# Written instruction order at the sublayer boundaries of a two-layer conditioned trunk

## The chip, the cores and the metric

The kernel runs on one core of a Trainium2 chip. The metric is device time in microseconds (us): the median of the runs shown. The profile is of one execution, with its own time.

## The reference, cut to what matters

Two layers, each three sublayers: a SwiGLU feed-forward (ffn), a token mixer (layer 0: the HGRN2 recurrence, "hg"; layer 1: a chunked gMLP, "gm"), and another ffn. 256 tokens, width 1024, ffn width 2816, all float32.

```python
def sublayer(x, fn, pre_g, post_g, shift, scale, gate, res_w):
    h = rms_norm(x, pre_g) * (1.0 + scale) + shift
    return x + res_w * gate * rms_norm(fn(h), post_g)

cond = jax.nn.silu(c)
for i in range(DEPTH):
    mod = (cond @ ada_w[i] + ada_b[i])      # 9 vectors of 1024: shift, scale, gate of 3 sublayers
    for s in range(N_SUB):
        x = sublayer(x, fns[s], norm_pre[i, s], norm_post[i, s],
                     mod[:, 3*s], mod[:, 3*s+1], mod[:, 3*s+2], (0.5, 1.0, 0.5)[s])
```

Between two sublayers lies a chain that no matmul of the next one can pass: norm of the product y, residual, norm of x, scale and shift to the next h.

## The kernel before, in words

**Tiles.** The 256 tokens are two tiles t of 128 rows. Every product is taken as three matmuls on float32 values split in a high and a low part: high by high, high by low, low by high. Activations h are kept transposed: h2[high or low, t, 128-column chunk].

**Weights.** They stream in as 188 blocks of two halves of 512 KB. A half is loaded by SyncE (SP) into a `raw` tile (four buffers), ScalarE (ACT) casts it to the high part (line 119, "the cast"), VectorE (DVE) subtracts that for the low part (line 120, "the sub"); both land in `whl` tiles (12 buffers). `next_block()` calls `wblock()` one or two blocks ahead of use.

**Ada.** The conditioning product is 144 column loads of 512 KB. Each is reduced against `cond` on DVE (line 169) into one column of `mod`. `pace()` gives each sublayer a number of blocks over which its share of these is spread.

**Units.** An ffn is 11 units of 256 columns: two input products, silu times product, a split in high and low, then the output product accumulated in y[t][h] (four PSUM banks, h the half of the width). `out_last()` does the output product of the last three units, 18 matmuls for each t and h; in hg it has 12. In hg, after the projections, `gate_f` (line 529 on) makes the decays in a tile `L`, a tree of levels fills the scores (lines 570 to 599), and the finish norms each head (lines 645 to 668: `ss`, `ots`) and multiplies by the output weights.

**The boundary.** `tail(t)` squares y (line 216, ACT), takes the root (line 79) and the reciprocal (line 224, DVE), multiplies y by the gate G (lines 259, 263), adds it to x (line 265). `nxt(t)` squares x, and `prenorm` scales it to `xn` (line 233 on DVE, 235 on ACT), transposes it on TensorE (PE) into `npa` (line 239), applies scale and shift on ACT in float32 (line 243), and splits it on DVE: a cast for the high part (line 247) and a subtraction for the low (line 248). Then `proj` (line 291 and on) starts the next sublayer. The boundaries are called B1 (ffn0 to hg), B2 (hg to ffn1), B3 (ffn1 to ffn2), B4 (ffn2 to gm) and B5 (gm to ffn3).

**Order.** `tile.TileContext(nc)` schedules the instructions of each engine; program order and tile dependences go in, and each engine runs its list in that order, one behind the other. Loads go out on SP's queue in program order.

Of the kernel before, what the change touches and what calls it, by code (L numbers as in the profile page):

```python
# [33 lines left out]
class Body:  # L34
    def __init__(self, ctx, tc, ins, out):
# [5 lines left out]
        self.whl = pool("whl", 12)  # L41
        self.act = pool("act", 1)
        self.adap = pool("adap", 2)
# [68 lines left out]
    def wblock(self, ap, n=2048):  # L112
        nc = self.nc
        hi, lo = self.wtile(), self.wtile()
        for h in range(2):
            sl = slice(h * n // 2, (h + 1) * n // 2)
            raw = self.raw.tile([P, 1024], F32, tag="raw", name="raw")[:, 0:n // 2]
            self.load(raw, ap[:, sl])
            nc.scalar.copy(hi[:, sl], raw)  # L119
            nc.vector.tensor_sub(lo[:, sl], raw, hi[:, sl])  # L120
        self.credit += self.rate
        while self.credit >= 1:
            self.credit -= 1
            self.ada(min(self.ada_next + 1, self.limit))
        return hi, lo

    def next_block(self):

        while len(self.ready) <= self.ahead and self.blk < len(self.blocks):
            self.ready.append(self.wblock(*self.blocks[self.blk]))  # L130
            self.blk += 1
        return self.ready.pop(0)
# [18 lines left out]
    def ada_setup(self):  # L151
        nc = self.nc
        self.ada_next = 0
        self.pace(0, 1)
        self.mod = [self.const.tile([P, 24], F32, name=f"mod{i}") for i in range(6)]
        self.cond = self.const.tile([P, D], F32, name="cond")
        self.ring = 0

    def ada(self, upto):
        nc = self.nc  # L160
        while self.ada_next < min(upto, 144):
            i = self.ada_next
            if self.ring and i % 3:
                t = self.p4.tile([P, D], F32, tag="t4", name="ada")
            else:
                t = self.adap.tile([P, D], F32, tag="ada", name="ada")
            self.load(t, self.d["ada"][i])
            junk = self.scr.tile([P, D], BF16, tag="junkv", name="junkv")
            nc.vector.tensor_tensor_reduce(junk, t, self.cond, 1.0, 0.0, ALU.mult, ALU.add,  # L169
                                           self.mod[i // 24][:, i % 24:i % 24 + 1])  # L170
# [38 lines left out]
    def rstd(self, src, second):  # L209

        nc = self.nc
        s2 = self.tiny.tile([P, 2], F32, tag="s2", name="s2")
        be = self.tiny.tile([P, 1], F32, tag="be", name="be")
        for h in range(2):
            junk = self.scr.tile([P, 512], BF16, tag="junka", name="junka")
            nc.scalar.activation(junk, src[h], AF.Square, accum_out=s2[:, h:h + 1])
            if h == 0:
                nc.vector.tensor_scalar(be, s2[:, 0:1], 1.0 / D, EPS, op0=ALU.mult, op1=ALU.add)
                if second is not None:
                    second()  # L220
        r = self.tiny.tile([P, 1], F32, tag="r", name="r")
        sq = self.tiny.tile([P, 1], F32, tag="sq", name="sq")
        self.tact(sq, s2[:, 1:2], AF.Sqrt, scale=1.0 / D, bias=be)
        nc.vector.reciprocal(r, sq)
        return r

    def prenorm(self, t, hT, A, sh, r):
        nc = self.nc
        xn = self.scr.tile([P, D], F32, tag="xn", name="xn")
        for h in range(2):  # L230
            hs = slice(h * 512, (h + 1) * 512)
            if h == 0:
                nc.vector.tensor_scalar(xn[:, hs], self.x[t][:, hs], r, None, op0=ALU.mult)
            else:
                nc.scalar.activation(xn[:, hs], self.x[t][:, hs], AF.Copy, scale=r)
            pa = self.yps.tile([P, 512], F32, tag=f"y{t}{h}", name="npa")
            for k in range(4):
                kc = 4 * h + k
                nc.tensor.transpose(pa[:, k * P:(k + 1) * P], xn[:, kc * P:(kc + 1) * P], self.ident)
            hf = self.scr.tile([P, 512], F32, tag="hf", name="hf")  # L240
            for k in range(4):
                kc = 4 * h + k
                nc.scalar.activation(hf[:, k * P:(k + 1) * P], pa[:, k * P:(k + 1) * P],
                                     AF.Identity, bias=sh[:, kc:kc + 1], scale=A[:, kc:kc + 1])
            hv = hf.rearrange("p (k t) -> p k t", k=4)
            hs4 = slice(4 * h, 4 * h + 4)
            nc.vector.tensor_copy(hT[0][:, t, hs4, :], hv)  # L247
            nc.vector.tensor_sub(hT[1][:, t, hs4, :], hv, hT[0][:, t, hs4, :])

    def tail(self, t, y, G, mm, nxt, last=False):  # L250

        nc = self.nc
        yg = self.scr.tile([P, D], F32, tag="yg", name="yg")
        xt = self.x[t]
        hs = [slice(0, 512), slice(512, D)]
        mm(t, 0)

        def second():
            nc.vector.tensor_mul(yg[:, hs[0]], y[t][0], G[:, hs[0]])
            mm(t, 1)  # L260

        r = self.rstd(y[t], second)
        nc.vector.tensor_mul(yg[:, hs[1]], y[t][1], G[:, hs[1]])
        for h in range(2):
            nc.vector.scalar_tensor_tensor(xt[:, hs[h]], yg[:, hs[h]], r, xt[:, hs[h]], op0=ALU.mult, op1=ALU.add)
            if last:
                self.load(self.out[t][:, hs[h]], xt[:, hs[h]])
        nxt(t)
# [10 lines left out]
    def proj(self, hT, wbs, n, split=False, kper=4):  # L279

        res = [[self.acc.tile([P, 512], F32, tag="acc", name="pps")[:, 0:n] for t in range(NT)] for _ in wbs]

        def go(g, t, blk):
            w = wbs[g][blk]
            ks = [blk * kper + k for k in range(kper)]
            h = lambda i, kc: hT[i][:, t, kc, :]
            u = lambda i, kc: w[i][:, (kc - ks[0]) * n:(kc - ks[0] + 1) * n]
            mm = self.nc.tensor.matmul
            if split:
                for kc in ks:  # L290
# [805 lines left out]
```

## Time and profile before

| what | value |
|---|---|
| runs | 1189.97, 1191.43, 1196.67 us; median 1191.43 |
| profiled execution | 1193.24 us, its span 1191.5 us |
| mean granted TensorE clock | 0.984 |
| PE, DVE, ACT busy | 96%, 75%, 55% of the span |
| moved by DMA | 282.32 MB, 237 GB/s over the span |

In a row of the table of windows stand the stretch, its length, then the busy time of each engine with its number of instructions, the granted TensorE clock (PEclk, 1.00 is full), the DMA share and rate. A row of the waits has the engine and what it wanted to do, what it waited for, the total in us, how often, and the longest. A row of the timeline has start and duration in us, engine, line, operation, output and input tiles, and in brackets the idle time before it with what ended it. A row of a group ends with total busy us, mean ns of one, and the idle time before it.

### The profile page before, as it was taken

How to read it: one execution, taken by the hardware profiler on the slowest of the kernel's cores; microseconds unless marked ns; L12 is line 12 of the kernel's file. 1: busy time of each engine (PE TensorE's matmuls, PEld its weight loads, DVE VectorE, ACT ScalarE, POOL GpSimd, SP SyncE). 2: the span in 40 equal slices, each digit the busy share in tenths (PEclk: the TensorE clock that was granted, in tenths of full speed). 3: DMA queues.
4: the chain of work that ended last, by engine and by line, in shares of the span. 5: the costliest groups of instructions: out<-in, count | busy, mean ns of one | idle time of the engine just before them, and what ended most of it. 6: DMA issues, size and time to landing. Idle time of an engine off the chain costs nothing.

```text
span 1191.5 us, 17180 instructions
## 1 busy us (share of the span) xinstructions
PE 1146.5 (96%) x6518; PEld 995.4 (84%) x6518; DVE 888.8 (75%) x1331; ACT 657.2 (55%) x1054; POOL 6.8 (1%) x16
## 2 busy tenths in 40 slices
PE   7999999997997999999999999999999999999997
PEld 6999998797895788888778888888888887888886
DVE  6997888868887887787677787657978786666652
ACT  6464446648766754456655545554754457555541
POOL 0000000000000000000000000000000000000000
PEclk9999999997999999999999999999999999999999
DMA  9899998782335777887578888537777765666640
GB/s 345 311 314 318 333 327 314 251 285 101 124 95 185 263 267 272 278 272 262 173 251 267 282 269 272 188 124 261 277 254 262 248 212 177 203 222 233 213 137 36
DMA packets 79765, 282.32 MB, mean 237 GB/s; under 512 B 9873, under 2 KB 10561, under 8 KB 79682
## 3 DMA queue, kind: packets, MB, share of 16 engines
q1 hardware_dynamic: 78626, 278.05, 68.0%
q0 software_dynamic: 1056, 3.17, 0.8%
q8 instruction: 51, 0.84, 0.3%
q14 instruction: 32, 0.26, 0.1%
HBM read 280.11 MB, written 1.07 MB: 236 GB/s over the span
## 4 chain that ended last, share of the span: by engine, by line
PE 73%; DMA 10%; DVE 8%; ACT 5%; issue 3%; SPq 0%; DVEq 0%; ACTq 0%
PE ups L328 15%; PE ups L329 8%; PE y L144 7%; PE y L142 7%; PE y L143 7%; PE ups L418 4%; DMA ada<-in_ada 4%; DMA raw<-in_wffn 4%; DVE w L120 3%; PE ups L334 3%; PE ups L336 3%; PE ups L335 3%; DMA raw<-in_whg 3%; ACT w L119 2%; PE ab L599 2%
## 5 line engine op out<-in xcount | busy, mean ns | idle before, releaser
L120 DVE TENSOR_TENSOR w<-raw,w 128x1024 fp32r<-128x1024 f32 x376 | 453.5, 1220 | 84.7 <-ACT w L119 77.5
L119 ACT CAST w<-raw 128x1024 fp32r<-128x1024 f32 x376 | 388.0, 1050 | 202.9 <-DMA raw<-in_wffn 79.4
L328 PE MATMUL ups<-h,w 128*128 128x512 f32 x864 | 303.1, 394 | 0.0
L169 DVE CUSTOM_DVE_ANT_0 junkv<-ada,cond 128x1024 bf16<-128x1024 f32 x144 | 175.8, 1221 | 92.0 <-DMA ada<-in_ada 91.5
L329 PE MATMUL ups<-h,w 128*128 128x256 f32 x864 | 242.5, 281 | 0.0
L328 PEld LDWEIGHTS ups<-h,w 128*128 128x128 f32 x864 | 162.3, 188 | 36.8
L142 PE MATMUL y<-w,t 128*128 128x512 f32 x448 | 179.4, 400 | 4.5 <-ACT t L147 4.5
L143 PE MATMUL y<-w,t 128*128 128x512 f32 x448 | 178.2, 398 | 0.0
L144 PE MATMUL y<-w,t 128*128 128x512 f32 x448 | 177.6, 397 | 0.2
L329 PEld LDWEIGHTS ups<-h,w 128*128 128x128 f32 x864 | 163.7, 190 | 0.9
L334 PE MATMUL ups<-h,w 128*128 128x256 f32 x416 | 118.3, 285 | 0.6 <-ACT w L119 0.6
L336 PE MATMUL ups<-h,w 128*128 128x256 f32 x416 | 117.8, 283 | 0.2 <-DVE w L120 0.2
L335 PE MATMUL ups<-h,w 128*128 128x256 f32 x416 | 117.6, 283 | 0.0
L142 PEld LDWEIGHTS y<-w,t 128*128 128x128 f32 x448 | 84.5, 189 | 24.1 <-ACT t L147 5.3
L144 PEld LDWEIGHTS y<-w,t 128*128 128x128 f32 x448 | 84.3, 189 | 21.0 <-DVE t L148 1.1
L143 PEld LDWEIGHTS y<-w,t 128*128 128x128 f32 x448 | 84.5, 189 | 17.9
L79 ACT ACTIVATE t<-t 128x256 f32<-128x256 f32 (+2 forms) x70 | 36.3, 523 | 97.7 <-DVE t L378 95.5
L334 PEld LDWEIGHTS ups<-h,w 128*128 128x128 f32 x416 | 79.7, 192 | 1.7 <-ACT w L119 0.8
L335 PEld LDWEIGHTS ups<-h,w 128*128 128x128 f32 x416 | 79.7, 192 | 0.8 <-issue 0.2
L336 PEld LDWEIGHTS ups<-h,w 128*128 128x128 f32 x416 | 79.7, 192 | 0.4 <-DVE w L120 0.4
L291 PE MATMUL pps<-w,h 128*128 128x512 f32 x160 | 64.4, 403 | 5.3 <-DVE h L247 5.3
L292 PE MATMUL pps<-w,h 128*128 128x512 f32 x160 | 63.8, 399 | 0.0
(199 smaller groups left out, 1435.4 us busy)
## 6 DMA issues: line engine op xcount, KB each, us to landing
raw<-in_wffn SPq DMA_DIRECT2D x264, 512.0 KB, 5.5
ada<-in_ada SPq DMA_DIRECT2D x144, 512.0 KB, 6.5
raw<-in_wgmu SPq DMA_DIRECT2D x48, 512.0 KB, 5.2
raw<-in_whg SPq DMA_DIRECT2D x40, 512.0 KB, 5.8
raw<-in_wgmv SPq DMA_DIRECT2D x24, 512.0 KB, 5.0
G<-gflat POOLq DMA_DIRECT2D x6, 512.0 KB, 5.9
t<-in_gbin SPq DMA_DIRECT2D x6, 256.0 KB, 5.2
x<-in_x SPq DMA_DIRECT2D x2, 512.0 KB, 4.0
```

The lines of the kernel that those rows point to most:

```text
L119: nc.scalar.copy(hi[:, sl], raw)
L120: nc.vector.tensor_sub(lo[:, sl], raw, hi[:, sl])
L142: self.paced(mm(ps, l[0], r[0], start=start, stop=False))
L143: mm(ps, l[0], r[1], start=False, stop=False)
L144: mm(ps, l[1], r[0], start=False, stop=stop)
L169: nc.vector.tensor_tensor_reduce(junk, t, self.cond, 1.0, 0.0, ALU.mult, ALU.add, self.mod[i // 24][:, i % 24:i % 24 + 1])
L291: mm(res[g][t], h(0, kc), u(0, kc), start=kc == 0, stop=False)
L328: self.paced(mm(ps, u[0], self.h2[:, :, :, kc, :], start=kc == 0, stop=False))
L329: mm(ps[:, 1, :], u[1], self.h2[:, 0, :, kc, :], start=False, stop=kc == KC - 1)
L334: self.paced(mm(o, u[0], h[0], start=start, stop=False))
L335: mm(o, u[0], h[1], start=False, stop=False)
L336: mm(o, u[1], h[0], start=False, stop=stop)
```

## The change

- All scheduling is done with `schedule_with_timeline_sim=True`. The five boundaries are written out by hand in `boundary()`, in a region in which ACT, DVE and PE keep the written order; `close()` ends it within the next sublayer. `tail()` remains for the end of the kernel.
- A weight half is now a `cast()` and a `sub()` that can be placed apart. `boundary()` sets four halves ahead of the last product of t0 (0, 0), two more between its halves, one cast and sub, and one more half, in t1's chain. Casts, subs and ada reduces that come later in the program are kept behind the last `h_high` and `h_low` by `hold`.
- ACT writes the high part of h directly from `npa` (`h_high`). DVE computes scale and shift again in float32, in four pieces of 128 columns, and subtracts (`h_low`).
- `proj` gives two lists, one for each tile, high by high and high by low first. The first 30 matmuls of t0 stand ahead of t1's transposes. In an ffn the first unit is interleaved with them (`first_units`).
- Ada loads are issued up to three reduces ahead at the start and have three buffers. `whl` has 14 buffers, and the reduce writes in place. `L` has a pool of its own. The paces go from 25 and 26 blocks to 23 and 22.
- In the finish of hg, by the order that results, the twelve output matmuls that stood behind the last heads' product `ab` on PE now stand ahead of it.

```diff
-        self.whl = pool("whl", 12)
+        self.whl = pool("whl", 14)
-        self.adap = pool("adap", 2)
+        self.adap = pool("adap", 3)
+        self.lp = pool("lp", 1)
...
+    def cast(self):
+        if self.half is None:
+            self.half = [self.wtile(), self.wtile(), 0]
+        hi, lo, h = self.half
+        ap, n = self.blocks[self.blk]
+        sl = slice(h * n // 2, (h + 1) * n // 2)
+        raw = self.raw.tile([P, 1024], F32, tag="raw", name="raw")[:, 0:n // 2]
+        self.load(raw, ap[:, sl])
+        self.after(self.nc.scalar.copy(hi[:, sl], raw), self.hold[0])
+        self.casts.append((hi, lo, sl, raw, h))
...
+    def sub(self):
+        hi, lo, sl, raw, h = self.casts.pop(0)
+        self.after(self.nc.vector.tensor_sub(lo[:, sl], raw, hi[:, sl]), self.hold[1])
...
+    def halves(self, n=1):
+        for _ in range(n):
+            self.cast()
+            self.sub()
...
-            junk = self.scr.tile([P, D], BF16, tag="junkv", name="junkv")
-            nc.vector.tensor_tensor_reduce(junk, t, self.cond, 1.0, 0.0, ALU.mult, ALU.add,
-                                           self.mod[i // 24][:, i % 24:i % 24 + 1])
+            for j in range(len(self.ada_tiles), min(i + (1 if self.ring else 3), 144)):
...
+                self.load(t, self.d["ada"][j])
+                self.ada_tiles.append(t)
+            t = self.ada_tiles[i]
+            self.after(nc.vector.tensor_tensor_reduce(t, t, self.cond, 1.0, 0.0, ALU.mult, ALU.add,
+                                                      self.mod[i // 24][:, i % 24:i % 24 + 1]), self.hold[1])
...
+    def h_high(self, t, h, xn, cols):
...
+        for k in range(4):
+            kc = 4 * h + k
+            last = nc.scalar.activation(self.h2[:, 0, t, kc, :], pa[:, k * P:(k + 1) * P], AF.Identity,
+                                        bias=sh[:, kc:kc + 1], scale=A[:, kc:kc + 1])
+        return pa, last
+
+    def h_low(self, t, h, pa, cols):
...
+        for k in range(4):
+            kc, ks = 4 * h + k, slice(k * P, (k + 1) * P)
+            nc.vector.tensor_scalar(hf[:, ks], pa[:, ks], A[:, kc:kc + 1], sh[:, kc:kc + 1],
+                                    op0=ALU.mult, op1=ALU.add)
+        hs4 = slice(4 * h, 4 * h + 4)
+        return nc.vector.tensor_sub(self.h2[:, 1, t, hs4, :], hf.rearrange("p (k t) -> p k t", k=4),
+                                    self.h2[:, 0, t, hs4, :])
...
+    def boundary(self, y, G, mm, cols, table):
+        self.region = self.tc.manual_schedule(engines={E.Activation, E.DVE, E.PE})
+        self.region.__enter__()
...
+        self.halves(4)
+        sy, sx, yg = self.row_stats(), self.row_stats(), ytile()
+        do(mm(0, 0))
+        sq(0, 0, sy)
+        self.half_mean(sy)
+        gated(0, 0, yg)
+        self.halves(2)
+        do(mm(0, 1))
+        sq(0, 1, sy)
+        gated(0, 1, yg)
+        r = self.inv_rms(sy)
+        self.residual(0, yg, r, sx)
+        r = self.inv_rms(sx)
+        do(mm(1, 0))
...
+        self.scaled(0, 0, xn, r)
+        sq(1, 0, sy1)
+        self.scaled(0, 1, xn, r)
+        self.half_mean(sy1)
+        gated(1, 0, yg1)
+        self.alloc_h()
+        m = mm(1, 1)
+        do(m[0:3])
+        pa0, _ = self.h_high(0, 0, xn, cols)
+        do(m[3:4])
+        pa1, _ = self.h_high(0, 1, xn, cols)
+        do(m[4:])
+        self.h_low(0, 0, pa0, cols)
+        self.h_low(0, 1, pa1, cols)
+        w = [[self.ready.pop(0) for _ in range(2)] for _ in range(2)]
+        self.res, go = self.proj(w)
+        sq(1, 1, sy1)
+        gated(1, 1, yg1)
+        r = self.inv_rms(sy1)
+        self.cast()
+        self.residual(1, yg1, r, sx1)
+        self.sub()
+        r = self.inv_rms(sx1)
...
+        self.halves(1)
+        p0 = go(0)
+        do(p0[0:30])
+        pa0, _ = self.h_high(1, 0, xn, cols)
...
+        self.table(table)
+        self.hold = (act, dve)
+        self.first = go(1)
...
-            L = self.adap.tile([P, 512], F32, tag="ada", name="L")
+            L = self.lp.tile([P, 512], F32, tag="L", name="L") if pr else self.scr.tile([P, 512], F32, tag="hf", name="L")
...
-    with tile.TileContext(nc) as tc:
+    with tile.TileContext(nc, schedule_with_timeline_sim=True) as tc:
```

What the change moves is seen in the lists of the engines. At the start of the kernel, on DVE before (the ISA rows are reduces: of x0 and x1 for the first norm, then of ada columns; `xn` and `yg` are the two tiles of normed x):

```order
L905 ISA xn,s_125<-x_99 128x1024
L905 ISA s_125 128x1
L905 ISA yg,s_125<-x_100 128x1024
L905 ISA s_125 128x1
L928 TENSOR_SCALAR ab_167<-adab 128x8
L907 TENSOR_SCALAR v<-s_125 128x2
L909 RECIPROCAL r<-v 128x2
L915 TENSOR_SCALAR xn<-x_99,r 128x512
```

and after:

```order
L1052 ISA xn,s_128<-x_102 128x1024
L1052 ISA s_128 128x1
L192 ISA ada,mod_106<-ada,cond 128x1024
L192 ISA mod_106 128x1
L1054 TENSOR_SCALAR v<-s_128 128x2
L192 ISA ada,mod_106<-ada,cond 128x1024
L192 ISA mod_106 128x1
L1091 TENSOR_TENSOR shift<-mod_106,adab 128x1
L1056 RECIPROCAL r<-v 128x2
L1092 SCALAR_TENSOR_TENSOR A<-mod_106,ab_170,npre 128x1
L1062 TENSOR_SCALAR xn<-x_102,r 128x512
```

Two ada reduces now stand ahead of the reciprocal and of xn. On ACT two weight casts moved from behind the first h to between the copies of the transposed x, and a third ahead of that h.

At B1, on ACT before (the CAST of t is the high part of the last unit of ffn0, y_797 and y_798 are y00 and y01):

```order
L147 CAST t_2037<-t_2036 128x512
L73 ACT_TABLE_LOAD
L119 CAST w<-raw 128x1024 x3
L216 ACTIVATE junka,s_2123<-y_797 128x512
L119 CAST w<-raw 128x1024
L216 ACTIVATE junka,s_2123<-y_798 128x512
L79 ACTIVATE sq<-s_2123,be 128x1
```

and after (y_784 and y_785):

```order
L167 CAST t_2009<-t_2008 128x512
L74 ACT_TABLE_LOAD
L122 CAST w<-raw 128x1024 x8
L235 ACTIVATE junka,s_2091<-y_784 128x512
L122 CAST w<-raw 128x1024 x2
L235 ACTIVATE junka,s_2091<-y_785 128x512
L80 ACTIVATE sq<-s_2091,be 128x1
```

Eight casts stand ahead of the first square instead of three, and two ahead of the second instead of one.

At B3, on DVE before (y_4081 and y_4082 are y00 and y01; `be` is half of the mean square):

```order
L218 TENSOR_SCALAR be<-s_5481 128x1
L259 TENSOR_TENSOR yg<-y_4081,G 128x512
L169 ISA junkv,mod_106<-ada,cond 128x1024
L169 ISA mod_106 128x1
L224 RECIPROCAL r<-sq 128x1
L263 TENSOR_TENSOR yg<-y_4082,G 128x512
L265 SCALAR_TENSOR_TENSOR x_99<-yg,r,x_99 128x512 x2
L218 TENSOR_SCALAR be<-s_5514 128x1
L224 RECIPROCAL r<-sq 128x1
L233 TENSOR_SCALAR xn<-x_99,r 128x512
```

and after (y_4097 and y_4098):

```order
L242 TENSOR_SCALAR be<-s_5429 128x1
L310 TENSOR_TENSOR yg<-y_4097,G 128x512
L132 TENSOR_TENSOR w<-raw,w 128x1024 x2
L310 TENSOR_TENSOR yg<-y_4098,G 128x512
L248 RECIPROCAL r<-sq 128x1
L255 SCALAR_TENSOR_TENSOR x_102<-yg,r,x_102 128x512
L242 TENSOR_SCALAR be<-s_5433 128x1
L255 SCALAR_TENSOR_TENSOR x_102<-yg,r,x_102 128x512
L248 RECIPROCAL r<-sq 128x1
L293 TENSOR_SCALAR xn<-x_102,r 128x512
```

The ada reduce ahead of the reciprocal is gone, and two weight subs stand between the two products with the gate.

More of the change, by code (lines that the diff above doesn't have):

```diff
@@ L110, in wtile, with wblock @@
         return self.whl.tile([P, 2048], dt, tag="w", name="w")
[L112 to L120, printed above, removed]
+    def cast(self):
[8 more added lines that the diff above has]
+        self.casts.append((hi, lo, sl, raw, h))
+        if h:
+            self.half, self.blk = None, self.blk + 1
+        else:
+            self.half[2] = 1
+    def sub(self):
+        hi, lo, sl, raw, h = self.casts.pop(0)
+        self.after(self.nc.vector.tensor_sub(lo[:, sl], raw, hi[:, sl]), self.hold[1])
+        if h:
+            self.ready.append((hi, lo))
+    def halves(self, n=1):
+        for _ in range(n):
+            self.cast()
+            self.sub()
+    def wblock(self):
+        self.halves(2)
         self.credit += self.rate
@@ new lines, in half_mean, with inv_rms, residual @@
+    def half_mean(self, st):
+        self.nc.vector.tensor_scalar(st[1], st[0][:, 0:1], 1.0 / D, EPS, op0=ALU.mult, op1=ALU.add)
+    def inv_rms(self, st):
+        s2, be, sq, r = st
+        self.tact(sq, s2[:, 1:2], AF.Sqrt, scale=1.0 / D, bias=be)
+        self.nc.vector.reciprocal(r, sq)
+        return r
+    def residual(self, t, yg, r, st=None):
+        for h in range(2):
+            hs = slice(512 * h, 512 * h + 512)
+            self.nc.vector.scalar_tensor_tensor(self.x[t][:, hs], yg[:, hs], r, self.x[t][:, hs],
+                                                op0=ALU.mult, op1=ALU.add)
+            if st is None:
+                self.load(self.out[t][:, hs], self.x[t][:, hs])
+            else:
+                self.square(self.x[t][:, hs], st[0], h)
+                if h == 0:
+                    self.half_mean(st)
@@ L214, in rstd, with close, tail @@
+    def close(self):
+        for op in self.first:
+            op()
+        self.region.__exit__(None, None, None)
+    def tail(self, t, y, G, mm):
+        yg = self.scr.tile([P, D], F32, tag="yg", name="yg")
+        st = self.row_stats()
         for h in range(2):
-            junk = self.scr.tile([P, 512], BF16, tag="junka", name="junka")
-            nc.scalar.activation(junk, src[h], AF.Square, accum_out=s2[:, h:h + 1])
+            for op in mm(t, h):
+                op()
+            self.square(y[t][h], st[0], h)
@@ L217, in rstd @@
             if h == 0:
[L218 to L268, printed above, removed]
+                self.half_mean(st)
@@ L335, in mm3f @@
         mm(o, u[0], h[1], start=False, stop=False)
[L336 removed]
+        self.last = mm(o, u[1], h[0], start=False, stop=stop)
     def gtile(self):
@@ L345, in out_unit @@
             for h in range(2):
+                self.gate = self.last
                 for k in range(2):
@@ L399, in post_tok @@
                     self.split_ps(*[g[:, :, t * P:(t + 1) * P] for g in gTs[u]], pv[:, u])
-            return gTs
+            act(0)
+            self.halves(2)
+            do(self.first[0:30])
+            ps = turn(0)
+            split(0, ps)
+            do(self.first[30:])
+            act(1)
+            wa, wb = nb(), nb()
+            steps = unit2(wa, wb)
+            next(steps)
+            ps = turn(1)
+            split(1, ps)
+            pend.extend(gTs)
+            next(steps)
+            self.first = []
+            self.close()
+            return steps
         def out():
@@ L789, in gelu, with tok @@
             self.tact(o, o, AF.Gelu_apprx_tanh)
+        def tok(n):
+            res = [self.acc.tile([P, 512], F32, tag="acc", name="pps")[:, 0:n] for t in range(NT)]
+            for b in range(2):
+                w = nb()
+                for t in range(NT):
+                    for k in range(4):
+                        kc = 4 * b + k
+                        self.mm3(res[t], [a[:, t, kc, :] for a in hT], [u[:, k * n:(k + 1) * n] for u in w],
+                                 kc == 0, kc == KC - 1)
+            return res
         v, vt = [], []
@@ L955, in run @@
         self.blocks, self.blk, self.ready, self.ahead = [], 0, [], 0
+        self.half, self.casts, self.hold = None, [], (None, None)
         for src, n, k in ((d["wffn"][0], 2048, 33), (d["whg"], 2048, 20), (d["wffn"][1], 2048, 33),
```

188 lines of the change are left out of this document (109 added, 79 removed).

## The prediction

> **What bounds the kernel now.** I read the engine totals first, then the table of windows around the sublayer boundaries, then PE's waits, and last the timeline of the places that wait.
>
> ```profile
> PE 1146.5 (96%) x6518; PEld 995.4 (84%) x6518; DVE 888.8 (75%) x1331; ACT 657.2 (55%) x1054; POOL 6.8 (1%) x16
> 360.93 0.48 PE L142 MATMUL y<-w 128*128 128x512 f32 x1
> ...
> 363.52 0.39 PE L144 MATMUL y<-w 128*128 128x512 f32 x1
> ```
>
> PE is the bound, and the number of matmuls is the same before and after, so only stretches in which PE stands still, or runs at half clock, can be won. The last two rows are the first and the last of twelve: (363.52 - 360.93) / 11 = 0.235 us for each 512-wide matmul when PE is fed. That is the unit in which I count cover.
>
> The windows below hold, in this order, the boundaries ffn0 to hg (B1), the front of hg, its finish, then hg to ffn1 (B2), ffn1 to ffn2 (B3), ffn2 to gm (B4) and gm to ffn3 (B5).
>
> ```profile
> core 0: us, PE busy (x) PEld busy (x) DVE busy (x) ACT busy (x) POOL busy (x), PEclk, DMA share, GB/s
> 204.00:222.00 18.00, 14.57 (x71) 11.54 (x70) 15.95 (x28) 13.14 (x27) 0.00 (x0) 1.00 0.67 222
> 268.00:294.00 26.00, 19.31 (x110) 18.49 (x109) 21.51 (x37) 24.70 (x48) 0.00 (x0) 0.74 0.33 116
> 362.00:373.00 11.00, 6.47 (x24) 4.53 (x23) 9.09 (x18) 7.74 (x20) 0.00 (x0) 0.84 0.69 238
> 381.00:393.00 12.00, 9.09 (x30) 6.73 (x29) 11.19 (x20) 11.28 (x26) 0.00 (x0) 0.72 0.30 93
> 573.00:615.00 42.00, 36.54 (x155) 28.71 (x154) 32.73 (x53) 28.83 (x54) 0.00 (x0) 0.92 0.63 216
> 766.00:800.00 34.00, 33.91 (x156) 27.27 (x155) 22.50 (x38) 22.45 (x48) 0.00 (x0) 1.00 0.33 109
> 1005.00:1025.00 20.00, 17.58 (x83) 13.39 (x81) 12.38 (x16) 13.30 (x22) 0.00 (x0) 1.00 0.61 210
> 577.00:580.40 3.40, 3.40 (x13) 3.01 (x13) 2.41 (x4) 3.40 (x7) 0.00 (x0) 0.50 0.00 0
> ```
>
> I count a window's loss as its PE idle time plus busy time times (1 - PEclk), since busy time at half clock is half lost:
> - B1: 18.00 - 14.57 = 3.4.
> - hg front: 6.7 idle + 19.31 x 0.26 = 11.7.
> - hg finish: 4.5 + 6.47 x 0.16 = 5.6.
> - B2: 2.9 + 9.09 x 0.28 = 5.5.
> - B3: 5.5 + 36.54 x 0.08 = 8.4.
> - B4: 0.1. B5: 2.4.
>
> Together 37 us, 3% of the span, is all that order can win besides the start. What PE waited for in them:
>
> ```profile
> PE ots L663 <- DVE t L658: 4.4, 1, 4.4
> PE npa L239 <- DVE xn L233: 3.2, 2, 2.1
> PE fps L336 <- DVE w L120: 3.1, 2, 1.7
> PE tps L396 <- DVE t L393: 0.9, 1, 0.9
> ```
>
> All of these are waits for DVE. Weights (line L120) are late only in the hg front; elsewhere the wait is for a norm's chain or a unit's product.
>
> **The change, part by part.**
>
> *The boundary chain.* After the change it has a fixed order. Its length comes from these groups:
>
> ```profile
> L216 ACT ACTIVATE junka<-y 128x512 bf16<-128x512 f32 x24 | 14.4, 598 | 39.0 <-PE y L144 38.9
> L216 ACT ACTIVATION_READ_ACCUMULATOR junka<-y 128x1 f32 x24 | 4.8, 200 | 0.0
> L79 ACT ACTIVATE sq<-s,be 128x1 f32<-128x1 f32 x22 | 6.6, 301 | 1.2 <-DVE be L218 0.7
> L224 DVE RECIPROCAL r<-sq 128x1 f32<-128x1 f32 x22 | 3.5, 157 | 4.3 <-ACT sq L79 4.2
> L265 DVE SCALAR_TENSOR_TENSOR x<-yg,r,x 128x512 f32<-128x512 f32 x24 | 17.0, 746 | 0.2
> L233 DVE TENSOR_SCALAR xn<-x,r 128x512 f32<-128x512 f32 x10 | 4.8, 485 | 0.3
> ```
>
> From the end of y00 (18 matmuls for each tile and half in an ffn): y01 ends at 18 x 0.235 = 4.2; square and its read 0.8, root 0.3, reciprocal 0.16, two residual halves 1.5, the square of the second half 0.8 behind them, root and reciprocal 0.46, xn 0.49: 8.7, and with some 0.1 us for each of ten hand-overs 9.7. PE has work until 4.2 + (18 + 9) x 0.235 = 10.6. So with free engines the transposes find xn ready.
>
> *B3.* Before, the chain took longer for a reason that the timeline shows:
>
> ```profile
> 569.77 0.29 ACT L79 ACTIVATE sq<-s,be 128x1 f32<-128x1 f32 x1
> 571.66 1.23 DVE L169 CUSTOM_DVE_ANT_0 junkv<-ada,cond 128x1024 bf16<-128x1024 f32 x1 [5.40 <-DMA ada<-in_ada]
> 572.81 0.16 DVE L224 RECIPROCAL r<-sq 128x1 f32<-128x1 f32 x1
> 576.83 1.84 PE L239 MATMUL npa<-ident,xn 128*128 128x128 f32 x8 [2.05 <-DVE xn L233]
> ```
>
> The root was done at 570.06; the reciprocal started at 572.81, since a reduce of an ada column stood ahead of it on DVE and DVE waited 5.40 us for that load. Those 2.75 us are PE's 2.05, and the half clock of 577.00:580.40 follows. The new order has no ada reduce there, and the two weight subs between the halves have their data long before. The t1 chain has 30 matmuls (7.1 us) against about 7.5 from y11: 0.5 stays. B3: 8.4 becomes 0.5, **-7.9**; ends 0 and -8.4. B4, with nothing to win, gets the same 0.5: **+0.4** (ends 0, +3). B5: 2.4 becomes 0.5, **-1.9** (ends 0, -2.4).
>
> *B2.* The last product of hg has 12 matmuls for each tile and half. From y01's end the chain takes 9.7 - 4.2 = 5.5, and two casts now stand between the squares; cover is (12 + 9) x 0.235 = 4.9. I put 1.9 on t0 and 2.1 on t1, 4.0 together, against 5.5 plus the 0.9 of the tps wait in the first unit, whose parts are now interleaved: **-2.4** (ends -6, +2).
>
> *B1.* Here a queue is too long. On ACT eight weight casts now stand between the last unit's cast and the square of y00, where three stood; two more stand ahead of the square of y01.
>
> ```profile
> 185.43 0.62 ACT L147 CAST t<-t 128x512 fp32r<-128x512 f32 x1 [0.58 <-DVE t L367]
> 186.07 1.28 ACT L73 ACT_TABLE_LOAD   x1
> 193.97 0.60 ACT L216 ACTIVATE junka<-y 128x512 bf16<-128x512 f32 x1 [1.92 <-PE y L144]
> raw<-in_whg SPq DMA_DIRECT2D x40, 512.0 KB, 5.8
> x<-in_x SPq DMA_DIRECT2D x2, 512.0 KB, 4.0
> L119 ACT CAST w<-raw 128x1024 fp32r<-128x1024 f32 x376 | 388.0, 1050 | 202.9 <-DMA raw<-in_wffn 79.4
> L120 DVE TENSOR_TENSOR w<-raw,w 128x1024 fp32r<-128x1024 f32 x376 | 453.5, 1220 | 84.7 <-ACT w L119 77.5
> ```
>
> Call y00's end 0: the table load ends at 187.35 - 193.95 = -6.6. Four casts run to -2.4. The raw tiles have four buffers, so the fifth load waits for the first sub, at -6.6 + 1.05 + 1.22 = -4.3, and lands 4.0 to 5.8 later (the median of these loads, and that of x, as large, on empty queues): -0.3 to 1.5. The eighth cast so ends at about 4.2 to 6.5, and the ninth and tenth, a buffer turn later, let the square of y01 start at 8.6 to 11 instead of 4.2: 4.4 to 7 late. Less the spare 0.9 of the chain, and with 0.6 on t1, PE loses about 5.5. A stall of that size may also halve the clock for 3.4 us, 1.7 more; in 204:222 single waits of up to 2.3 left PEclk at 1.00, in B3 a wait of 2.05 did not, so I add a quarter of it, 0.4. B1: 3.4 becomes 5.9, **+2.5**; ends -2.5 (loads found early) and +5.3 (late loads and half clock).
>
> The Trainium skill, "TensorE: Matmul & The Clock Gate" (the section on HAM oscillation), says to have no PE-idle gaps over about 3.4 us, since an idle window puts the clock back to half. By that rule B1's stall is long enough to be sure of the half clock, and the sum would be 1.3 us higher; the B3 row, half clock after a gap of 2.05 us, does not agree with the length of gap it names.
>
> *hg front.* The gate's tile L leaves the buffers of the ada loads:
>
> ```profile
> L529 ACT ACTIVATE L<-fps 128x512 f32<-128x512 f32 x4 | 2.4, 591 | 4.0 <-DVE mod L169 3.9
> ```
>
> That wait of 3.9 goes, and the f weights (the fps wait) come early enough. But DVE is busy 21.51 of 26 us there, so it paces the rest. I take **-3.4**; ends 0 and -9.
>
> *hg finish.* The twelve y matmuls from 360.93 to 363.52, which covered the norm of the last heads, now stand ahead of the product that this norm reads. Behind them PE waited:
>
> ```profile
> 368.29 1.94 PE L663 MATMUL ots<-ident,t 128*128 128x128 f32 x7 [4.38 <-DVE t L658]
> ```
>
> Their 12 x 0.235 = 2.8 are added to the wait: **+2.8**; ends 0 and +6, the latter if the subs ahead of the mean wait for raw buffers too.
>
> *Start.* DVE now does two ada reduces ahead of the reciprocal, ACT two weight casts among the copies:
>
> ```profile
> 6.32 1.22 DVE L905 CUSTOM_DVE_ANT_0 xn<-x 128x1024 f32<-128x1024 f32 x1 [5.33 <-PE cps L897]
> 9.37 0.49 DVE L915 TENSOR_SCALAR xn<-x,r 128x512 f32<-128x512 f32 x1
> 11.69 1.67 ACT L922 COPY w<-xps 128x512 f32<-128x512 f32 x3
> 15.99 6.19 PE L418 MATMUL ups<-h,w 128*128 128x256 f32 x37 [2.41 <-ACT h L950]
> ```
>
> The two reduces take 2.6, of which 0.3 fell into DVE's wait for the root: xn 2.3 late. The copies begin 1.0 behind xn instead of 1.8, -0.8. Two more casts ahead of the first h, +2.0. The first product starts 3.5 later and PE then has no slack up to B1: **+3.5**; ends +1.5 and +5.
>
> *The rest.* Half of h's low part: 80 small multiply-adds replace 20 casts on DVE. Between the 485 ns of the xn row (512 columns) and the 157 ns of the reciprocal (one column) I estimate 0.23 us each, +10 us of DVE work in all, hidden behind at least 16 matmuls (3.8 us) in each tile; uncovered it would cost those 10. The reduce now writes f32 in place: L905 above does just that in 1.22, so nothing. Fourteen weight buffers, three ada loads ahead and the new paces change a lead that ACT (202.9 us idle at L119) and DVE had anyway: 0, ends -2 and +3. The end of the kernel keeps its code.
>
> **The sum.** 3.5 + 2.5 - 3.4 + 2.8 - 2.4 - 7.9 + 0.4 - 1.9 = -6.4. The profiled execution took 1193.2 (its span 1191.5), 1.8 over the median of 1191.4, so 1186.8 in its own terms and **1185.0** against the median, -0.5%.
>
> **The rivals.**
> - *Everything fits.* Loads land early, so B1 ends at 0.9 (-2.5), B2 at 1.4 (-5), the finish costs nothing, the front gives 3.9: 3.5 - 2.5 - 3.9 - 5 - 7.9 + 0.1 - 1.9 = -17.6, **1174**. For it: the chain is 9.7 against 10.6. Against it: the buffer turn at B1.
> - *Slower: raw buffers inside the written order.* If the casts placed between the squares wait for loads at B2 to B5 as at B1, each loses 5.9: 23.6 against 17.3 now (with the tps wait), +6.3, and with start, B1, front and finish (+5.4) +11.7, **1203**. It decides from (17.3 - 5.4) / 4 = 3.0 us for each boundary; over that the kernel is slower. Against it: at B3 no cast stands between the last unit and y00's square.
> - *The stalls move.* DVE paces the hg front as now (0) and the finish costs 6: 3.5 + 2.5 + 6 - 2.4 - 7.9 + 0.4 - 1.9 = +0.2, **1192**. For it: DVE's 21.51 of 26 us.
>
> **How the numbers follow.** Forecast 0.43, everything fits 0.18, slower 0.17, moved 0.22. About 0.5%, 6 us, is what a measurement here tells from no change. The forecast's own range is 1178 to 1192, cut at 1185.5 near its middle. Faster: 0.18 + 0.24 + 0.03 = 0.45; slower: 0.17 + 0.06 of the moved = 0.23; same 0.32. The range runs from the first rival to short of the second, with the bounds of start and front: 1171 to 1201.
>
> **What would show it.** Right: the first 256-wide product at about 19.5; no PE wait over 1 us within B3 and no half clock behind it; at B1 the square of y00 some 4 us behind y00 and a wait of about 5 before the first npa; an ots wait of some 7; the wait of L for mod gone. Wrong: half clock behind B2 or B5, ACT casts waiting for raw between two squares there, or new PE waits for weights inside ffn0, where the lead is smallest.

## The result and the profile after

The changed kernel takes 1211.51 us (median of 4 runs, 1210.55 to 1212.96) against 1193.13 of the kernel before beside it: ratio 1.0163, 95% interval [1.0138, 1.0188]. It is slower by 1.6%; 1185 was forecast, between 1171 and 1201. The profiled execution has a span of 1211.2 against 1191.5.

The totals, from the page of the changed kernel:

```profile
PE 1146.2 (95%) x6518; PEld 999.8 (83%) x6518; DVE 908.3 (75%) x1391; ACT 664.4 (55%) x1054; POOL 6.8 (1%) x16
```

PE does the same work as before; 20 us more of waiting and half clock lie around it. DVE has 19.5 us more. What PE waits for, from the list of waits of the changed kernel (total us, how often, the longest):

```profile
PE ab L741 <- ACT t L80: 9.8, 1, 9.8
PE npa L271 <- DVE xn L293: 8.2, 5, 2.4
PE ots L805 <- DVE t L800: 7.4, 1, 7.4
PE npa L271 <- DVE be L242: 6.7, 2, 5.1
PE y L162 <- ACT t L167: 6.0, 2, 3.4
PE xps L1068 <- DVE xn L1062: 5.6, 1, 5.6
PE vps L1003 <- ACT w L1001: 4.5, 1, 4.5
```

A row names the waiting product and what it waited for. The waits of the old boundary for the high cast of h and for the late weights of the f gate are gone. The wait for xn stands once at each boundary, 8.2 us together against 4.9 before. Beside it stand a few long ones: the first product of hg's tree (`ab`), the finish of hg (`ots`), the first npa at B1 and B2 (`be`), and two inside gm (`vps`, `y`). Only the two inside gm were not in the forecast in any form.

To see where time is lost, not only where PE waits, I compare the start times of matmuls at equal amounts of PE work (each matmul counted at its full-rate interval by width). The table is worked out from the traces: lag behind the kernel before, in us, when the same work is done. "All, model" is the changed kernel; the other columns are experiments told below.

| place (time in the kernel before) | all, model | all, default | hybrid, default | hybrid, model | none, default | before, model | ada 40 |
|---|---|---|---|---|---|---|---|
| inside ffn0 (113) | 3.2 | -0.9 | -0.6 | 2.0 | -0.1 | 2.3 | 2.8 |
| behind B1 (231) | 6.8 | 6.1 | 0.4 | 19.1 | 0.7 | 13.9 | 0.6 |
| hg, weights of f in (283) | -0.2 | -0.9 | -6.7 | 12.0 | -6.4 | 6.8 | -5.8 |
| hg, tree under way (330) | 6.4 | 12.0 | -7.3 | 9.2 | -7.2 | 5.1 | 5.8 |
| behind the finish (381) | 10.1 | 12.5 | -5.1 | 14.5 | -4.8 | 8.8 | 9.3 |
| inside ffn1 (443) | 7.9 | 10.6 | -8.5 | 13.1 | -3.2 | 27.5 | 6.7 |
| behind B3 (651) | 0.7 | 2.1 | -17.0 | 7.9 | -10.2 | 34.3 | 0.4 |
| behind B4 (799) | 3.8 | 3.6 | -16.9 | 10.9 | -10.1 | 45.8 | 3.6 |
| gm, v half done (850) | 4.3 | 9.8 | -16.9 | 10.9 | -10.1 | 45.1 | 2.5 |
| gm, first u units (870) | 12.8 | 10.5 | -15.7 | 20.4 | -9.9 | 58.9 | 9.9 |
| gm, last units (993) | 21.8 | 8.3 | -14.4 | 27.9 | -6.2 | 65.1 | 17.3 |
| inside ffn3 (1105) | 19.7 | 6.3 | -16.5 | 26.3 | -6.4 | 78.9 | 15.3 |

A column tells of one place by the step from one row to the next: a rise is a loss there, a fall a gain. Of the 19.7 us of the changed kernel, 18.0 arise between B4 and the last units of gm, where no boundary is. There the timeline of the changed kernel shows DVE in the chain of the layer norm (`nm` is its last link, which the ACT scaling at L1001 and then the vps product need):

```profile
857.16 1.22 DVE L132 TENSOR_TENSOR w<-raw,w 128x1024 fp32r<-128x1024 f32 x1
858.30 0.21 DVE L96 SCALAR_TENSOR_TENSOR rs_q<-rs_y,rs_hv 128x1 f32<-128x1 f32 x1
858.43 1.22 DVE L132 TENSOR_TENSOR w<-raw,w 128x1024 fp32r<-128x1024 f32 x1
859.56 0.16 DVE L101 SCALAR_TENSOR_TENSOR rs_y<-rs_q,rs_y 128x1 f32<-128x1 f32 x1
...
862.00 1.22 DVE L192 CUSTOM_DVE_ANT_0 ada<-ada,cond 128x1024 f32<-128x1024 f32 x1
863.14 0.08 DVE L192 DVE_READ_ACCUMULATOR2_ANT mod<- 128x1 f32 x1
...
863.21 0.15 DVE L983 SCALAR_TENSOR_TENSOR nm<-mv,rr 128x1 f32<-128x1 f32 x1
```

Links of 0.2 us alternate with weight subs and ada reduces of 1.2 us. In the list of the kernel before four subs stand between the first tile's aggregate and its nm, in that of the changed kernel six subs and two ada reduces. Later in gm DVE stands at ada loads:

```profile
946.75 1.23 DVE L192 CUSTOM_DVE_ANT_0 ada<-ada,cond 128x1024 f32<-128x1024 f32 x1 [3.96 <-DMA ada<-in_ada]
...
960.16 1.23 DVE L192 CUSTOM_DVE_ANT_0 ada<-ada,cond 128x1024 f32<-128x1024 f32 x1 [4.99 <-DMA ada<-in_ada]
...
963.87 0.48 DVE L1010 SCALAR_TENSOR_TENSOR t<-vps,glng,bc 128x256 f32<-128x256 f32 x1
```

The L1010 step, which a unit of gm needs, stands behind three reduces, the first of which waited 4.99 us for its load. DVE's waits in gm, first the changed kernel (800 to 1000 us), then the one before (790 to 990):

```profile
DVE ada L192 <- DMA ada<-in_ada: 26.1, 7, 5.1
```

```profile
DVE junkv L169 <- DMA ada<-in_ada: 10.5, 7, 3.1
```

It is the same kind of wait that made B3 slow before, and gm has 15.6 us more of it. Over the whole run DVE waits less for ada loads than before, 44.9 us against 91.5; what changed is that more of the waiting falls where PE needs DVE.

### The profile page after: what moved, and what is told of

Same layout as the page of the kernel before. It is cut to its first block, busy times and chain, and to the rows that moved or that the text cites. A ratio compares the mean times of both kernels' runs of the same rounds, so it can differ in the third digit from the quotient of the medians.

```text
span 1211.2 us, 17149 instructions
## 1 busy us (share of the span) xinstructions
PE 1146.2 (95%) x6518; PEld 999.8 (83%) x6518; DVE 908.3 (75%) x1391; ACT 664.4 (55%) x1054; POOL 6.8 (1%) x16
## 3 DMA queue, kind: packets, MB, share of 16 engines
q1 hardware_dynamic: 78626, 278.05, 65.1%
## 4 chain that ended last, share of the span: by engine, by line
PE 76%; DVE 9%; DMA 7%; ACT 5%; issue 3%; SPq 0%; DVEq 0%; ACTq 0%
PE ups L437 15%; PE ups L438 8%; PE y L162 8%; PE y L163 8%; PE y L164 8%; PE ups L557 4%; PE pps L412 4%; PE ups L443 4%; PE ups L445 4%; PE ups L444 4%; DVE w L132 3%; DMA raw<-in_wffn 3%; DVE hf L284 2%; PE ab L741 2%; DMA raw<-in_wgmu 1%
## 5 line engine op out<-in xcount | busy, mean ns | idle before, releaser
L192 DVE CUSTOM_DVE_ANT_0 ada<-ada,cond 128x1024 f32<-128x1024 f32 x144 | 174.3, 1222 | 45.0 <-DMA ada<-in_ada 44.9
L412 PE MATMUL pps<-w,h 128*128 128x512 f32 x480 | 115.1, 396 | 0.2 <-DVE h L287 0.2
L162 PEld LDWEIGHTS y<-w,t 128*128 128x128 f32 x448 | 85.6, 191 | 25.9 <-ACT t L167 6.7
L412 PEld LDWEIGHTS pps<-w,h 128*128 128x128 f32 x480 | 89.8, 190 | 19.1 <-DVE h L287 0.7
L164 PEld LDWEIGHTS y<-w,t 128*128 128x128 f32 x448 | 84.8, 189 | 21.8 <-DVE t L168 1.7
L163 PEld LDWEIGHTS y<-w,t 128*128 128x128 f32 x448 | 85.7, 191 | 18.3
L167 ACT CAST t<-t 128x512 fp32r<-128x512 f32 x50 | 31.1, 622 | 66.9 <-DVE t L498 30.2
```

Source lines behind the costliest of these rows:

```text
L162: self.paced(mm(ps, l[0], r[0], start=start, stop=False))
L163: mm(ps, l[0], r[1], start=False, stop=False)
L164: mm(ps, l[1], r[0], start=False, stop=stop)
L192: self.after(nc.vector.tensor_tensor_reduce(t, t, self.cond, 1.0, 0.0, ALU.mult, ALU.add, self.mod[i // 24][:, i % 24:i % 24 + 1]), self.h ...
L412: lambda g=g, i=i, j=j, kc=kc, w=w: mm(res[g][t], h2[:, i, t, kc, :], w, start=kc + i + j == 0, stop=i == 1 and kc == KC - 1)))
```

## The experiments

Three theories stood at first. S: the timeline model orders the instructions outside the written parts worse than the default scheduler. L: the ada loads and paces of the change cost the time. B: the written boundaries shift the work of gm.

**1. All written boundaries, default scheduler.**

```diff
-    with tile.TileContext(nc, schedule_with_timeline_sim=True) as tc:
+    with tile.TileContext(nc) as tc:
```

> The changed kernel with the scheduling of the rest as before: TileContext without the timeline model, all written boundaries, loads and paces kept. Theory S (the model's order of DVE inside gm, with weight subs and ada reduces between the links of the layer-norm chain and of the last units, costs the 18 us there): the loss inside gm goes, and the time is about 1193, down to 1185 if the hg front is also better ordered. Theory L (the ada loads and paces of the change cost it): stays near 1211. Theory B (the written boundaries shift the work in gm): stays near 1211.

Measured 1198.53, ratio to before 1.0049 [1.0023, 1.0075]: 13 us less than the changed kernel, still slower than before. From the v half's end (850) on the lag falls by 3.5 instead of rising by 15.4, and the start is 0.9 ahead of before instead of 3.2 behind. Theory S holds for these; but B1 costs more still (7.0 against 3.6), and gm's v half loses 6 (3.6 to 9.8).

**2. The kernel before with the model.** `TileContext(nc, schedule_with_timeline_sim=True)` alone.

> The kernel before with one edit: the timeline model schedules it; no written boundary, loads and paces as before. Theory S: gm loses much as in the changed kernel, total 1205 to 1215. Theories L and B: no loss in gm, within 5 us of 1193.

Measured 1269.38, ratio 1.0653 [1.0620, 1.0685]. The expectation was far too small. gm loses 19 here too (45.8 to 65.1), and the rest of the kernel, most of it the boundaries, which have no written order here, 60. DVE's waits for ada loads over the whole run, here and before:

```profile
DVE junkv L169 <- DMA ada<-in_ada: 130.1, 61, 6.0
```

```profile
DVE junkv L169 <- DMA ada<-in_ada: 91.5, 51, 5.4
```

**3. The ada part undone.** Loads at their own reduce, two buffers, paces 25 and 26.

```diff
-            for j in range(len(self.ada_tiles), min(i + (1 if self.ring else 3), 144)):
+            for j in range(len(self.ada_tiles), min(i + 1, 144)):
```

> The changed kernel with the ada part undone: each load issued at its own reduce, two buffers, paces 25 and 26. Theory L: gm's 18 us go, about 1193. Theories S and B: gm still loses 12 or more; the total is 1206 to 1213, the start perhaps 2 us shorter.

Measured 1219.78, ratio 1.0227 [1.0185, 1.0269]: slower than the changed kernel by 8. Theory L falls: gm still loses 14.8 (8.7 to 23.5 by the same comparison). Loads, buffers and paces were undone together, so the run says that the three together help, and not which of them.

**4. The layer-norm chain of gm alone held together.** Behind its last link `self.hold = (self.hold[0], last)`.

> The changed kernel with one place in gm put in written order: weight subs and ada reduces that come later in the program are held behind the last link of the layer-norm chain (line 983), so that nothing of 1.2 us stands between its links. Theory S: the wait of 4.6 us for the normed v at 860 and the half clock behind it go, 5 to 8 us, total 1203 to 1207; the other losses in gm at 950 to 1000 stay. Theories L and B: under 2 us, since the subs held back then make the weights of the first u units late.

Measured 1213.14, ratio 1.0181 [1.0151, 1.0210]: nothing gained. PE's waits in 800:1000 of this run:

```profile
PE y L162 <- ACT t L167: 5.5, 3, 4.2
PE ups L445 <- DVE w L132: 5.1, 1, 5.1
PE vps L1004 <- DVE t L1011: 2.8, 2, 2.5
```

The wait for the normed v (4.5) is gone, and a wait of 5.1 for a weight sub that stood behind the chain has come in its place. Whichever part is put first makes the other late, and my expectation of 5 to 8 us was wrong. It is not shown that the links were well placed as they were: the hold also kept subs behind the chain, and DVE stands idle for 4.39 us just before the chain (2.19 in the changed kernel). With the default scheduler (experiment 1) one sub stands between the first tile's aggregate and its nm, not six, and 0.7 us are lost from 850 to 870 instead of 8.5, though that run had lost 6 just before.

**5. gm's ada reduces out of the v half** (on top of experiment 1): `self.pace(bg, 24, 12)` for `self.pace(bg, 30, 6)`.

> The kernel with the default scheduler and the written boundaries (the first experiment), with one edit: in gm no ada reduce comes in the first 12 weight blocks (the v half) instead of the first 6, so that none stands on DVE ahead of the weight subs there. Theory Q (DVE waits for ada loads at the head of its queue at 825 to 832 while landed weights stand behind, and the 7 us that gm's front loses follow from it): 4 to 7 us shorter, about 1192 to 1194, with no wait of PE for subs at 834 to 857. Theory D (DVE is simply full there with the work that the written boundary moved): less than 2 us.

Measured 1202.58, ratio 1.0093 [1.0066, 1.0119]; the lag still rises by 8.6 from 819 to 870 (6.9 in experiment 1). The run doesn't decide on theory Q, since the new pace left the wait in place that it was meant to take out. Two reduces still stand there on DVE, and the first waits for its load as long as before. First experiment 1, with the step of the v half behind the two and what PE waits for then; below it this run:

```profile
833.63 1.23 DVE L192 CUSTOM_DVE_ANT_0 ada<-ada,cond 128x1024 f32<-128x1024 f32 x1 [5.37 <-DMA ada<-in_ada]
...
836.08 0.69 DVE L924 TENSOR_TENSOR w<-pps,t 128x512 f32<-128x512 f32 x1
836.83 0.27 PE L219 MATMUL gps<-ident,gate 128*8 128x128 f32 x1 [1.84 <-DVE w L924]
```

```profile
833.79 1.22 DVE L192 CUSTOM_DVE_ANT_0 ada<-ada,cond 128x1024 f32<-128x1024 f32 x1 [5.24 <-DMA ada<-in_ada]
```

So the rows speak for theory Q rather than against it: DVE's wait of 5.37 ends in PE's wait of 1.84. No run took this wait out by itself.

**6. The hybrid: default scheduler, written order at B2, B3 and B5 only.**

```diff
+                    go = self.boundary if s in (1, 2, 4) else self.plain
+                    go(y, G, mm, st["cols"], tables[subs[s + 1][0]])
```

`plain` is the former tail and prenorm.

> Default scheduler; the written boundary only at B2, B3 and B5, the former code at B1 and B4 (with the former cast and subtraction for h there). From the ledger of the first experiment B1 (+8.4) and B4 (+1.9) should fall to 0 and B2, B3, B5 keep -2, -8.6 and -2; gm's front (+6.9) goes only if it came from the written B4. If every term stands by itself: 1176 to 1184, faster than before by 0.7 to 1.3%. If losses only move (DVE late elsewhere): within 6 us of before.

Measured 1177.83, ratio 0.9881 [0.9859, 0.9903], against 1190.42 before beside it: faster than both kernels, and within the expected 1176 to 1184. The losses of experiment 1 at B1, in the front of hg and in gm's v half are all gone. As only the boundaries B1 and B4 differ, the written B1 and B4 together are their cause. By the place, B1 made the tree of hg late (from 283 to 330 experiment 1 loses 12.9, the hybrid gains 0.6), and B4 the v half; no run wrote one of the two alone. In the v half of the hybrid the longest wait of DVE for an ada load is under 3 us. Why a written B1 reaches so far is seen in the windows behind it, 205:225 and 265:295, first of experiment 1, then of the hybrid, which has the same scheduler, and last of the changed kernel (PE, PEld, DVE, ACT, POOL busy, PEclk, DMA share, GB/s):

```profile
205.00:225.00 20.00, 13.55 (x53) 11.19 (x54) 13.35 (x30) 12.59 (x32) 0.00 (x0) 0.74 0.30 108
...
265.00:295.00 30.00, 24.93 (x182) 24.75 (x181) 29.54 (x50) 26.47 (x49) 0.00 (x0) 0.85 0.72 244
```

```profile
205.00:225.00 20.00, 17.17 (x76) 13.68 (x76) 20.00 (x36) 16.42 (x34) 0.00 (x0) 0.91 0.90 291
...
265.00:295.00 30.00, 28.91 (x224) 28.20 (x222) 25.76 (x41) 27.57 (x51) 0.00 (x0) 0.94 0.39 129
```

```profile
205.00:225.00 20.00, 14.20 (x61) 11.15 (x60) 13.84 (x29) 12.34 (x31) 0.00 (x0) 0.91 0.37 128
...
265.00:295.00 30.00, 20.25 (x163) 20.04 (x161) 29.09 (x52) 27.80 (x53) 0.00 (x0) 0.87 0.79 276
```

With the written chain no ada reduce runs in 205:225 (the hybrid spends 7.1 us of DVE on them there), and the DMA share is 0.30 for 20 us instead of 0.90 (0.37 in the changed kernel). My reading is that work held behind the chain keeps its buffers, so the loads stop. The reduces not done then come later: in 265:295 they take 5.9 us in experiment 1, 7.3 in the changed kernel and nothing in the hybrid. There DVE is busy 29.54 and 29.09 of 30 us, and hg's tree needs it; PE's waits for `ab` are the price, 6.6 and 5.1 us in experiment 1, 9.8 in the changed kernel. That the held work is what fills DVE there is read from these rows; no run tried the written B1 without the hold.

**7. Six raw buffers.** `pool("raw", 6)`, and to make room `pool("whl", 13)`.

> The changed kernel with six raw buffers instead of four and 13 weight buffers instead of 14; the written order on ACT and DVE at B1 is the same. If the four raw buffers hold up the ten casts ahead of the second square: the stall of 5.3 before the first npa at B1 falls below 2, B1 gives back 3 to 5 us, and the other boundaries change little: 1204 to 1209. If the ten casts themselves are too long (10.5 us of ACT): B1 keeps 4 or more.

Measured 1252.43, ratio 1.0496 [1.0463, 1.0530]. It tells nothing on the raw buffers by themselves, since a weight buffer was given up with them and the time got worse. All five boundaries now have the same wait, and in B3 DVE stands 8.15 us at the sub between the halves:

```profile
PE npa L271 <- DVE be L242: 32.5, 5, 6.5
```

```profile
592.63 2.36 DVE L132 TENSOR_TENSOR w<-raw,w 128x1024 fp32r<-128x1024 f32 x2 [8.15 <-issue]
```

That sub's casts had ended at 585.6, and in the list it waits for PE too, so with 13 buffers its target is most likely one that a product late in the boundary still reads; the trace names no releaser. Fourteen buffers, which I had put at 0 in the prediction, may be what makes the written order possible at all.

**8. B1 with a lead.** `"ffn0": 40` for 46 ada columns in ffn0.

> The changed kernel with 40 instead of 46 of the ada columns in ffn0 (the six go to hg): 7.7 us less of loads ahead of B1, and the order that results has two casts ahead of the first square of B1 instead of eight. Theory W (at B1 the weights have no lead, so the casts that the next product needs queue up ahead of the square and each waits a turn of four raw buffers): the stall of 5.3 before the first npa falls under 1.5, and B1's loss of 4.1 turns into a gain of 1 to 4; hg may lose up to 4 by its six more reduces. Total 1205 to 1211. Theory C (the written chain at B1 is too long in itself): the stall stays over 4.

Measured 1209.73, ratio 1.0143 [1.0105, 1.0181]. The stall of 5.1 before the first npa at B1 is gone, and B1 turns from a loss of 3.6 into a gain of 2.2 (2.8 to 0.6). In hg it is given back. PE's waits in 195:300 of the changed kernel and then of this run:

```profile
PE ab L741 <- ACT t L80: 9.8, 1, 9.8
PE npa L271 <- DVE be L242: 5.1, 1, 5.1
PE npa L271 <- DVE xn L293: 0.7, 1, 0.7
```

```profile
PE ab L741 <- ACT t L80: 14.8, 1, 14.8
PE npa L271 <- DVE xn L293: 1.6, 1, 1.6
```

Theory W holds at B1. The 5 us that B1 gave up were added to the wait for `ab`: the tree of hg is paced by DVE, and PE only comes to it earlier. The six reduces that this run moves into hg add to DVE's work there too; the run doesn't part the two.

**9. The hybrid with the model.** One flag against experiment 6.

> The hybrid of the sixth experiment (written boundary at B2, B3, B5; former code at B1, B4) with the timeline model as scheduler instead of the default: one flag against it. Theory S (the model's order outside the written parts is the loss): 20 to 45 us slower than the hybrid, 1198 to 1222, with the loss at B1, hg, B4 and in gm from 830 on. If the model only harms together with the written B1 and B4: within 6 us of 1178.

Measured 1219.45, ratio 1.0209 [1.0170, 1.0249]: 42 us more than the hybrid. It loses at the start, at B1 (17), and in gm (10.9 to 27.9), as theory S says. Under the model the written B1 of the changed kernel is the better one (3.6 against 17), so what is said of B1 in experiment 6 holds for the default scheduler. DVE waits 22.2 us for ada loads in 800:1010; the hybrid, with the default scheduler, 6.5 in 770:970:

```profile
DVE ada L192 <- DMA ada<-in_ada: 22.2, 8, 5.0
```

```profile
DVE ada L192 <- DMA ada<-in_ada: 6.5, 6, 2.9
```

**10. No written boundary, default scheduler.** `plain` at all five, everything else of the change kept.

> Default scheduler, no written boundary at all (former boundary code at all five), all the rest of the change kept: ada loads ahead, 14 weight buffers, L in its own tile, paces, interleaved first unit. By the hybrid's ledger the rest gives about 10 us in the front of hg and the written B2, B3, B5 about 8: expected 1183 to 1189. If the written boundaries give all of the hybrid's gain: 1188 to 1194.

Measured 1187.14, ratio 0.9956 [0.9937, 0.9976]. So the rest of the change is worth 5 us, most of it in the front of hg, and the written B2, B3 and B5 another 9 (hybrid 1177.83).

**11. gm without ada, and 12. the hybrid without ada in gm.** `"ffn2": 138` for 118, in the changed kernel and in the hybrid.

> The changed kernel with all of gm's twenty ada columns moved to ffn2 (138 instead of 118 done there), so that no ada load or reduce is left in gm. In the changed kernel DVE waits 26.1 us for ada loads between 800 and 1000 (before 10.5, with the default scheduler 7.6). Theory H (the model's order sets ada reduces at the head of DVE's queue before their loads land, and gm's loss is those waits): gm gives back 9 to 15 of its 18 us, total 1197 to 1204, ffn2 unchanged. Theory O (it is the order among subs, layer-norm links and last units, whatever waits): gm gives back under 5 us, total 1207 to 1213; PE still waits about 4 us for the normed v and 3 to 4 us for the last unit's t.

> The hybrid (default scheduler, written boundary at B2, B3, B5) with gm's ada columns moved to ffn2 as well. The hybrid still loses 4 us at PE's waits for vps chains between 826 and 890. Theory H: 1 to 4 us shorter than the hybrid's 1177.8. If the ada work is hidden in gm there: within 2 us of it; longer if 46 loads in ffn2 disturb B4.

Measured 1216.71 (ratio 1.0199 [1.0149, 1.0249]) and 1194.84 (1.0017 [0.9996, 1.0038]). In the first, gm loses 8.2 (16.6 behind B4 to 24.8 at its last units) instead of 18.0, so 9.8 hang on the ada work in gm; the rest stays with the order, since PE still waits for the normed v and for the last unit's t (780:1010):

```profile
PE npa L271 <- DVE be L242: 7.2, 1, 7.2
PE vps L1003 <- ACT w L1001: 4.3, 1, 4.3
PE y L162 <- ACT t L167: 2.8, 1, 2.8
```

But the first row of these is B4, which now has the trouble of B1: twenty more loads in ffn2 leave the weights no lead, and ffn2, from its first unit to B4, loses 12 more than in the changed kernel. In the hybrid the same move costs 17 us: from 680 to 780, in ffn2, the DMA share is 0.88 and PE busy for 87.80 of 100 us. The hybrid's row, with 0.59 and 99.82, stands below it:

```profile
680.00:780.00 100.00, 87.80 (x425) 71.89 (x426) 81.31 (x118) 57.50 (x95) 1.08 (x2) 0.96 0.88 309
```

```profile
680.00:780.00 100.00, 99.82 (x492) 82.89 (x492) 65.97 (x95) 55.58 (x97) 1.07 (x2) 1.00 0.59 199
```

These two runs move the ada loads and don't remove them, so the share of gm's loss that hangs on the ada work is read from the lag within gm alone.

## Why the prediction was wrong

Its terms against the lag that each place added (forecast, measured):

| term | forecast | measured |
|---|---|---|
| start | +3.5 | +3.2 |
| B1 | +2.5 | +3.6 |
| hg front | -3.4 | -0.4 |
| hg finish | +2.8 | +3.7 |
| B2 | -2.4 | -2.2 |
| B3 | -7.9 | -7.2 |
| B4 | +0.4 | +3.1 |
| gm inside | 0 | +18.0 |
| B5 | -1.9 | -2.1 |

The step that failed is the paragraph on the rest, which gave everything outside the boundaries 0, ends -2 and +3; gm alone measured +18.0. I had followed the new list at the five boundaries, the start and hg, and taken the other stretches to be harmless because weights were cast well ahead of use. The scheduler's flag reorders those as well. Lead covers a late weight; it does not cover a link of a chain that stands behind a reduce whose load has not landed. With the default scheduler gm loses 4.7 in place of 18.0 (experiment 1 against the changed kernel) and 2.5 in place of 17.0 (experiments 6 and 9), so the model's order costs 13 to 15 us there. With gm's ada work moved away, gm loses 9.8 less (experiment 11). What within the model puts the reduces there was not tried.

The same paragraph had a second term too small. The 80 multiply-adds for the low part of h took 27.3 us in place of the 8.5 of the 20 casts, so DVE got 18.8 us more work there and not 10, nearly all of the 19.5 that its total grew. What this cost in time no run shows by itself. That the reduce in place costs nothing came out (1.22 us as before), though L905, the row it was read from, does not write in place.

At the start the forecast was met in part by luck: the first product came at 18.54, 2.6 us later than before and not 3.5. The rest of the 3.2 was lost behind it, where the matmuls ran slow up to 24.50 (28 in 5.96 us, 0.21 each, against 0.12 for the same width later) and before only up to 20.63.

Most boundary steps came out as written. B3: the ada reduce ahead of the reciprocal was the wait, and with it the half clock is gone; one wait of 1.6 remains at t1, by this row, which is over the 0.5 forecast:

```profile
594.48 0.65 PE L271 MATMUL npa<-ident,xn 128*128 128x128 f32 x4 [1.58 <-DVE xn L293]
```

B1: the turn of four raw buffers shows in the casts, each waiting for its load, the square of y00 (L235) behind the eighth:

```profile
196.48 1.05 ACT L122 CAST w<-raw 128x1024 fp32r<-128x1024 f32 x1 [2.57 <-DMA raw<-in_whg]
...
199.05 1.06 ACT L122 CAST w<-raw 128x1024 fp32r<-128x1024 f32 x1 [1.52 <-DMA raw<-in_whg]
200.62 1.05 ACT L122 CAST w<-raw 128x1024 fp32r<-128x1024 f32 x1 [0.51 <-DMA raw<-in_whg]
...
202.77 0.59 ACT L235 ACTIVATE junka<-y 128x512 bf16<-128x512 f32 x1
```

Experiment 8 bears out that the lead of the weights decides at B1; that it is four buffers and not some other number was not tested by itself. B4 was mis-sized: a wait of 2.0 at t1 and half clock behind it (PEclk 0.91 in 778:798) where 0.5 was put down. At B1 the half clock came: PEclk is 0.91 in 205:225, behind a gap of 5.1 us. This agrees with the Trainium skill's rule on gaps ("TensorE: Matmul & The Clock Gate", HAM oscillation), but does not single it out. The hybrid has the same 0.91 there behind a gap of 2.33 us, and the kernel before, with a gap of 2.27 at the same place, none. The first row is the hybrid's, the second that of the kernel before:

```profile
211.00:215.00 4.00, 4.00 (x13) 3.10 (x11) 4.00 (x7) 3.87 (x9) 0.00 (x0) 0.57 0.94 321
```

```profile
211.00:215.00 4.00, 4.00 (x19) 3.29 (x18) 4.00 (x8) 2.35 (x7) 0.00 (x0) 1.00 0.60 219
```

So the length of the gap alone does not tell here whether the clock halves.

hg front: the weights did come 7 us earlier, as forecast, but DVE paced what follows and took all of it back. I had seen DVE's 21.51 of 26 us and used it only to trim the gain. The rival "the stalls move" had that mechanism right; its price was too small, since held work had been added to DVE's load, as far as the rows of experiment 6 show it; without a written B1 (experiment 10) the front keeps its gain. hg finish: 12 matmuls moved ahead gave a wait of 7.4, as the sum 4.4 + 2.8 had it.

The slower rival (1203) rested on raw buffers at B2 to B5. That did not happen at B2, B3 and B5, which kept their gains, and the loss came from a place that no rival named.

## What to carry to other kernels

When a change swaps the scheduler, every stretch has a new order; read the whole list against the old one, and look first for waits for loads at the head of a queue. An order written by hand pays where the operands are there already (B3) and costs where loads have no lead (B1, and B4 with more loads ahead); by the rows of experiment 6, holding work back also stops the loads behind it. Choose it place by place. The best version here keeps the default scheduler and writes three of five boundaries: 1.2% faster than before.

## What the runs showed of the hardware that was not expected

With the written order at one boundary the DMA share was 0.30 for 20 us instead of 0.90 under the same scheduler, and DVE was busy 29.54 of 30 us some 60 us later. Two gaps of PE of nearly the same length at the same place, 2.33 and 2.27 us, were followed by half clock in one run and by full clock in the other. A multiply-add of 128 columns on DVE, put at 0.23 us, took 0.34 (27.3 us for 80). One weight buffer less out of 14, with two raw buffers more, cost 41 us over the changed kernel.
